# One layer of a hybrid decoder: Winograd block products with both x parts in one 512-column moving operand, and sums moved to GpSimd

## Chip, cores and metric

The kernel runs on one core of one Trainium2 chip. The metric is the device time of the program in microseconds (us); shorter is better. The engines are TensorE (PE, with its weight loads as PEld), VectorE (DVE), ScalarE (ACT), GpSimd (POOL) and SyncE (SP); SP and POOL also issue the DMAs.

## The reference

512 tokens, width 1024, one layer in float32. A mixer (stick-breaking attention and a gated short convolution, merged by two sigmoid gates), a cross-attention into 256 memory tokens, then a SwiGLU feed-forward of hidden size 2816, each with a residual, and a final norm. What the change touches is the projections of the last two sublayers:

```python
q = (h @ w_q).reshape(b, s, MEM_HEADS, MEM_HEAD_DIM)
...
hf = rms_norm(x, norm_ffn[l])
gate, up = jnp.split(hf @ w_ffn_in[l], 2, axis=-1)
x = x + (jax.nn.silu(gate) * up) @ w_ffn_out[l]
```

## The kernel before

**Two parts.** Every float32 operand of a matmul is split in two reduced parts, hi (a cast on ScalarE) and lo (the value less hi, a subtraction on VectorE). A product then takes three matmuls: hi by hi, hi by lo, lo by hi.

**Block products.** Three projections (the last merge gates, the memory queries, the FFN's input weights) use Winograd's scheme for 2x2 blocks: seven products (i = 0 to 6) of block sums instead of eight plain ones. For the FFN, block m of 22 makes 128 gate and 128 up channels for 512 tokens; the four memory-query blocks have numbers QM to QM + 3, the gate blocks start at GM. The x side is split by halves of the tokens (HS = 256 columns) and by pairs of 128-row chunks (four pairs, KP). `odd_forms` and `even_forms` (L605 to L636) make the seven forms of x for a pair, each 256 columns, as hi and lo: three tiles of 512 columns for oh, ch, dh with their lows, and u. The weight side is four raw blocks of 512 columns loaded per m plus sums of them.

**Loads.** `ffn_load(m)` (L712) issues three SP loads (s13, wg, a22) and, on POOL, a DMA that adds two blocks onto s13. `ffn_raw(m, i)` (L729) makes the two remaining sums (i = 3 and 6), each a 128x512 add; its engine is VectorE unless the call says GpSimd, which it does for the few sums ahead of a stage. `ffn_form(m, i)` (L741) casts a raw block on ScalarE and subtracts on VectorE; products 0 and 1 share one of 1024 columns.

**Products and banks.** `product(ps, m, i)` (L768) issues for each of four k three matmuls of 256 columns. The products of one m use three PSUM banks: z for i = 0, 3, 4, 5, v for 1, y for 2 and 6. Products 3 to 6 accumulate onto what is in the bank, so what was there must be read first. `reads(m, i)` (L794) does so: ScalarE copies z after 0, 3 and 4 (and after 5 for memory queries), VectorE adds v or y to a copy. `second(m)` (L807) adds y, as product 2 left it, to the copy of product 4. Half of every bank (256 columns) is used.

**Order.** `order(m0, n)` (L812) interleaves two neighbouring m: (m,3), (m+1,0), (m,4), (m+1,1), (m,5), (m+1,2), (m,6), and so on; the seven products from one such group to the next are called a block here. The FFN loop (L1159 to L1218) is under a manual schedule, in which PE, ACT and DVE run their instructions as written; POOL is not in the list. At step n the loop issues product n, its reads, the form of the product AHEAD = 6 steps on, and the sum of the one SUM_AHEAD = 2 steps further. `evict` (L1107) then multiplies the gate half by the norm's factor (L1111), applies SiLU on ScalarE, and multiplies by the up half, read in two halves from z and from the copy (L1118). Steps with i = 3 and m from 2 to 9 also scale a chunk of x2T for the final residual (L1201). The FFN's output product comes after (L1268), with `turn` products (L1287) over part of it that use `act_forms`.

**Pools.** xpool and upool hold the forms of x; tpool the copies and gate tiles; wpool and fpool the weights. The raw sums and a22 share a ring of four buffers (tag w2).

Of the kernel before, what the change touches and what calls it, by code (L numbers as in the profile page):

```python
# [50 lines left out]
def hybrid_layer(ctx: ExitStack, tc: tile.TileContext, xT_d, memT_d, cols_d, wv_d, win_d,  # L51
# [560 lines left out]
    def odd_forms(u, c, xe, xo, last=None):  # L612
        lo, hi = slice(0, HS), slice(HS, S)
        d = f(unit("c2"))
        oh, ol, ch, cl = (unit(t) for t in ("xoh", "xol", "xch", "xcl"))
        dh, dl = (last or spare)("xdh"), (last or spare)("xdl")
        nc.scalar.copy(oh, xo)
        nc.vector.tensor_tensor(out=c[:, hi], in0=xo[:, hi], in1=xe[:, hi], op=ALU.subtract)
        nc.vector.scalar_tensor_tensor(out=d[:, lo], in0=c[:, lo], scalar=-1.0, in1=xo[:, hi],  # L619
                                       op0=ALU.mult, op1=ALU.subtract)  # L620
# [5 lines left out]
        nc.vector.tensor_tensor(out=cl, in0=c, in1=f(ch), op=ALU.subtract)  # L626
        nc.vector.tensor_tensor(out=dl, in0=d, in1=f(dh), op=ALU.subtract)
        return listed((u[:, lo], u[:, hi]), oh, ol, ch, cl, dh, dl)

# [82 lines left out]
    def ffn_load(m):  # L712

        src = (wfi_d[m] if m < NF else wfp_d[m - NF] if m < QM else wmq_d[m - QM] if m < GM
               else wga_d[m - GM])
        a = src.rearrange("p (i c) -> p i c", i=4)
        s13, wg = ((fpool, "wg") if (m % 3, t) in ((1, "ws"), (2, "wg")) else (wpool, "wr")
                   for t in ("ws", "wg"))
        s13 = s13[0].tile([P, 2, 512], F32, tag=s13[1], name=nm("ws"))
        after(nc.sync.dma_start(s13, a[:, 2:3, :].broadcast_to([P, 2, 512])), x_loads[-1:])  # L720
        wg = wg[0].tile([P, 2, 512], F32, tag=wg[1], name=nm("wg"))
        nc.sync.dma_start(wg, a[:, 0:2, :])
        a22 = fpool.tile([P, 512], F32, tag="w2", name=nm("a22"), bufs=4)
        nc.sync.dma_start(a22, a[:, 3, :])
        nc.gpsimd.dma_start(s13, a[:, 0:4:3, :], accum_op=ALU.add)  # L725
        pairs[m] = wg
        raws[m] = [wg[:, 0, :], wg[:, 1, :], s13[:, 1, :], None, s13[:, 0, :], a22, None]

    def ffn_raw(m, i, eng=nc.vector):  # L729
        if m not in raws:  # L730
            ffn_load(m)
        w = raws[m]
        if w[i] is None:
            w[i] = fpool.tile([P, 512], F32, tag="w2", name=nm("s2"), bufs=4)
            a, b = (w[2], w[0]) if i == 3 else (w[3], w[1])
            eng.tensor_tensor(out=w[i], in0=a, in1=b, op=ALU.add)
        return w[i]
# [30 lines left out]
    def product(ps, m, i, ks=range(KP)):  # L768

        w = wforms[m, i]  # L770
        for k in ks:
            hi, lo = (w[j][:, k * P:(k + 1) * P] for j in range(2))
            xh, xl = (x2f if m < NF else af if m < QM else x1f if m < GM else x0f)[k][i]
            for j, (a, b) in enumerate(((hi, xh), (hi, xl), (lo, xh))):
                nc.tensor.matmul(ps[:, :HS], a, b, start=i < 3 and k == 0 and j == 0,  # L775
                                 stop=k == KP - 1 and j == 2, skip_group_check=True)

    banks, act, silus, stts = {}, {}, [], []

    def bank_of(m, i, new=True):  # L780
        if not new:
            pass
        elif i == 0:
            banks[m] = {"z": ztile("z"), "s": None if m >= GM else tmp("sa"),
                        "t": f(unit("qb")) if QM <= m < GM else tmp("sb")}
        elif i == 1:
            banks[m]["v"] = mmtile("v")
            if m < GM:
                banks[m]["g"] = f(unit("qa")) if m >= QM else tmp("fg")
        elif i == 2:  # L790
            banks[m]["y"] = otile("y")
        return banks[m]["zvyzzzy"[i]]

    def reads(m, i):  # L794

        b = banks[m]
        z, s, t = b["z"][:, :HS], b["s"], b["t"]
        if i in (0, 3, 4) or i == 5 and m >= QM:
            nc.scalar.copy((s[:, :HS], None, None, s[:, HS:], t[:, :HS], t[:, :HS])[i], z)  # L799
        elif i == 1:  # L800
            nc.vector.tensor_tensor(out=b["g"][:, :HS], in0=b["v"][:, :HS], in1=s[:, :HS],
                                    op=ALU.add)
        elif i == 6:
            nc.vector.tensor_tensor(out=b["g"][:, HS:], in0=b["y"][:, :HS], in1=s[:, HS:],
                                    op=ALU.add)

    def second(m):  # L807
        b = banks[m]
        nc.vector.tensor_tensor(out=b["t"][:, HS:], in0=b["y"][:, :HS], in1=b["t"][:, :HS],
                                op=ALU.add)  # L810

# [295 lines left out]
    def evict(m, part):  # L1107
# [6 lines left out]
        else:  # L1114
            a = act[m] = f(unit("act"))
            for half, u in enumerate((b["z"][:, :HS], b["t"][:, HS:])):
                sl = slice(half * HS, (half + 1) * HS)
                stts.append(nc.vector.scalar_tensor_tensor(out=a[:, sl], in0=u, scalar=-1.0,  # L1118
                                                           in1=g[:, sl], op0=ALU.mult,
                                                           op1=ALU.mult))  # L1120

# [37 lines left out]
    with tc.manual_schedule(engines={mybir.EngineType.PE, mybir.EngineType.Activation,  # L1159
                                     mybir.EngineType.DVE}):  # L1160
        ahead = uses[:3] + [(1, 0)]
# [4 lines left out]
        for n, (m, i) in enumerate(uses):  # L1166
            if (m, i) == (1, 0):
                product(banks[m]["z"], m, i, range(KP - 2, KP))
            elif n > 2:
                product(bank_of(m, i), m, i)  # L1170
            if i == 4:
                reads(m, i)
            elif i == 5 and m == NF - 1:
                reads(m, i)
                second(m)
            else:
                if i == 1 and m > 0:
                    second(m - 1)
                reads(m, i)
            if i == 5 and TURN_AT <= m < TURN_AT + KD:  # L1180
# [106 lines left out]
    def turn_product(p, i):  # L1287
# [180 lines left out]
```

## Time and profile before

| | before |
|---|---|
| time of three runs | 2944.97, 846.79, 846.61 us; median 846.79 |
| the profiled execution's own time | 847.03 us |
| its span, first to last instruction | 845.3 us |
| mean granted TensorE clock | 0.997 |
| HBM read, written | 116.42 MB, 2.10 MB |
| FFN products, from the first to the last | about 498 to 724 us |
| memory-query products | about 342 to 383 us |

A profile is one execution. In its rows a tile is named without its buffer number, and a line can be that of a helper that many callers share: the product matmuls of all stages are L775. Durations of neighbouring instructions of one engine overlap a little, so the pitch from start to start says more of the engine's load than the duration. "Idle before" is time that the engine stood still ahead of an instruction, with what ended it.

### The profile page before, as it was taken

The page shows a single profiled execution, that of the slowest core. Times are in us where ns is not written, and L with a number is a line of the kernel's source. Part 1 is how long each engine was busy: PE and PEld are TensorE (multiplying, and loading weights), DVE is VectorE, ACT ScalarE, POOL GpSimd, SP SyncE. Part 2 cuts the span into 40 slices and gives each one's busy share as a digit, 9 for nine tenths or more (in the row PEclk, how much of TensorE's full clock was granted, in tenths as well). Part 3 has the DMA queues.
Part 4 walks back from the last instruction along what each step waited for, and adds up shares of the span by engine and source line. Part 5 has one row for each costly group of instructions (what it writes and reads, how often), then busy time and mean ns, then how long its engine had stood idle before and what let it go on. Part 6 is the DMA issues. An engine that isn't in the chain of part 4 may idle for free.

```text
span 845.3 us, 13478 instructions
## 1 busy us (share of the span) xinstructions
PE 835.7 (99%) x5095; PEld 748.2 (89%) x5095; DVE 669.3 (79%) x1152; ACT 482.9 (57%) x873; POOL 88.5 (10%) x113
## 2 busy tenths in 40 slices
PE   9999999999999999999999999999999999999996
PEld 7888787888899988999988899999999999888885
DVE  8769889987856867978775889888877778895764
ACT  7556767566534555766554766555455556554434
POOL 1011112210100011000000111211111110110013
PEclk9999999999999999999999999999999999999998
DMA  8332332314745484555331437777777763870112
GB/s 299 128 122 64 108 104 66 111 51 167 206 104 146 148 251 128 162 178 194 129 115 56 112 86 202 189 185 177 179 182 178 180 156 125 269 216 26 51 50 100
DMA packets 50257, 120.47 MB, mean 143 GB/s; under 512 B 5136, under 2 KB 8208, under 8 KB 50192
## 3 DMA queue, kind: packets, MB, share of 16 engines
q1 hardware_dynamic: 40656, 101.49, 36.2%
q0 software_dynamic: 9248, 17.83, 13.0%
q8 instruction: 40, 0.66, 0.3%
q10 hardware_dynamic: 288, 0.29, 0.1%
q14 instruction: 25, 0.20, 0.1%
HBM read 116.42 MB, written 2.10 MB: 140 GB/s over the span
## 4 chain that ended last, share of the span: by engine, by line
PE 99%; DVE 0%; ACT 0%; issue 0%; DVEq 0%; ACTq 0%
PE z L775 20%; PE y L775 10%; PE pr L176 6%; PE pr L177 6%; PE pr L178 6%; PE v L775 5%; PE r L176 3%; PE r L178 3%; PE r L177 3%; PE f L177 3%; PE f L176 3%; PE f L178 3%; PE v L282 3%; PE br L177 2%; PE br L176 2%; PE br L178 2%
## 5 line engine op out<-in xcount | busy, mean ns | idle before, releaser
L167 ACT CAST wh<-wr 128x1024 fp32r<-128x1024 f32 x82 | 85.6, 1048 | 51.8 <-PE pr L177 11.3
L170 DVE TENSOR_TENSOR wl<-wr,wh 128x1024 fp32r<-128x1024 f32 x82 | 99.9, 1222 | 18.7 <-ACT wh L167 17.9
L775 PE MATMUL z<-xdh,wf 128*128 128x256 f32 x480 | 94.6, 282 | 0.0
L176 PE MATMUL pr<-xgh,wh 128*128 128x512 f32 x224 | 87.8, 392 | 0.0
L178 PE MATMUL pr<-xgh,wl 128*128 128x512 f32 x224 | 87.3, 390 | 0.0
L177 PE MATMUL pr<-xgl,wh 128*128 128x512 f32 x224 | 87.3, 390 | 0.0
L775 PEld LDWEIGHTS z<-xdh,wf 128*128 128x128 f32 x480 | 77.5, 189 | 0.3 <-issue 0.2
L775 PE MATMUL z<-xdl,wf 128*128 128x256 f32 x240 | 67.0, 279 | 0.0
L799 ACT COPY sa<-z 128x256 f32<-128x256 f32 x52 | 19.4, 373 | 74.1 <-PE z L775 74.0
L766 DVE TENSOR_TENSOR wf<-s,wf 128x512 fp32r<-128x512 f32 x60 | 41.4, 691 | 22.8 <-ACT wf L765 21.6
L725 POOL DMA_DIRECT2D ws<-in_w_ffn_in_dram x22 | 26.5, 1203 | 299.0 <-DVE c L619 109.5
L752 DVE TENSOR_TENSOR wf<-wg,wf 128x1024 fp32r<-128x1024 f32 x30 | 36.8, 1226 | 18.1 <-ACT wf L749 18.1
L178 PEld LDWEIGHTS pr<-xgh,wl 128*128 128x128 f32 x224 | 42.0, 188 | 8.9
L176 PEld LDWEIGHTS pr<-xgh,wh 128*128 128x128 f32 x224 | 42.1, 188 | 8.6 <-DVE rv L135 0.3
L177 PEld LDWEIGHTS pr<-xgl,wh 128*128 128x128 f32 x224 | 42.1, 188 | 8.3
L775 PE MATMUL y<-xch,wf 128*128 128x256 f32 x240 | 49.0, 286 | 0.0
L775 PE MATMUL z<-xch,wf 128*128 128x256 f32 x240 | 48.1, 283 | 0.0
L775 PEld LDWEIGHTS z<-xdl,wf 128*128 128x128 f32 x240 | 45.4, 189 | 0.2
L177 PE MATMUL f<-wl,acth 128*128 128x512 f32 (+1 forms) x116 | 44.3, 382 | 0.0
L176 PE MATMUL f<-wh,acth 128*128 128x512 f32 (+1 forms) x116 | 44.3, 382 | 0.0
L178 PE MATMUL f<-wh,actl 128*128 128x512 f32 (+1 forms) x116 | 44.1, 382 | 0.0
L766 DVE TENSOR_TENSOR wf<-ws,wf 128x512 fp32r<-128x512 f32 x60 | 40.9, 682 | 1.4 <-ACT wf L765 1.3
(357 smaller groups left out, 2466.3 us busy)
## 6 DMA issues: line engine op xcount, KB each, us to landing
wr<-in_w_in_dram SPq DMA_DIRECT2D x28, 512.0 KB, 3.5
ws<-in_w_ffn_in_dram SPq DMA_DIRECT2D x22, 512.0 KB, 3.8
ws<-in_w_ffn_in_dram POOLq DMA_DIRECT2D x22, 512.0 KB, 5.8
wg<-in_w_ffn_in_dram SPq DMA_DIRECT2D x22, 512.0 KB, 4.2
wr<-in_w_ffn_out_dram SPq DMA_DIRECT2D x14, 512.0 KB, 4.4
a<-in_w_ffn_in_dram SPq DMA_DIRECT2D x22, 256.0 KB, 4.4
wr<-in_w_branch_dram SPq DMA_DIRECT2D x8, 512.0 KB, 3.5
wr<-in_w_mix_out_dram SPq DMA_DIRECT2D x8, 512.0 KB, 3.7
```

What stands on the lines that cost most here:

```text
L167: after(nc.scalar.copy(h2, raw), lead[-1:] + waiting[:1])
L170: lows.append(nc.vector.tensor_tensor(out=l2, in0=raw, in1=f(h2), op=ALU.subtract))
L176: nc.tensor.matmul(ps, a[0], b[0], start=start, stop=False, **kw)
L177: nc.tensor.matmul(ps, a[0], b[1], start=False, stop=False, **kw)
L178: nc.tensor.matmul(ps, a[1], b[0], start=False, stop=stop, **kw)
L282: nc.tensor.matmul(vps[t], xg[k][a][:, sl], wv[k][b], start=k == 0 and (a, b) == (0, 0), stop=k == KD - 1 and a == 1)
L725: nc.gpsimd.dma_start(s13, a[:, 0:4:3, :], accum_op=ALU.add)
L752: nc.vector.tensor_tensor(out=lo, in0=pair, in1=f(hi), op=ALU.subtract)
L766: nc.vector.tensor_tensor(out=lo, in0=raw, in1=f(hi), op=ALU.subtract)
L775: nc.tensor.matmul(ps[:, :HS], a, b, start=i < 3 and k == 0 and j == 0, stop=k == KP - 1 and j == 2, skip_group_check=True)
L799: nc.scalar.copy((s[:, :HS], None, None, s[:, HS:], t[:, :HS], t[:, :HS])[i], z)
```

## The change

`odd_forms` lays every form of x out as one 512-column tile: hi in the left half, lo in the right; it casts and subtracts in six pieces of 256 columns. `product` then issues, for FFN and memory queries, one matmul of hi with the whole 512 columns and one of lo with the 256 of xh. So the bank's left half holds hi xh + lo xh and its right half hi xl, and the two halves must be added. `reads` copies or adds banks at their full width into two-part tiles (g2 for the gate half, t2 for the up half, of the new pool twopool; z is now copied after product 5 too), and `fold` adds left and right halves on GpSimd. `evict` takes the folded up half in one instruction. The FFN's weight sums move from VectorE to GpSimd. POOL enters the FFN's manual schedule: the load of m + 2 stands at (m,1), sum 3 of m + 1 at (m,2), sum 6 of m + 2 at (m,6). The a22 load is issued apart, when its form comes near. The last two lines make the buffer that POOL's DMAs use smaller. The gate blocks keep three matmuls; the turn products use the first two entries of a form.

```diff
+    twopool = ctx.enter_context(tc.tile_pool(name="twopool", bufs=1))
...
     def odd_forms(u, c, xe, xo, last=None):
         lo, hi = slice(0, HS), slice(HS, S)
         d = f(unit("c2"))
-        oh, ol, ch, cl = (unit(t) for t in ("xoh", "xol", "xch", "xcl"))
-        dh, dl = (last or spare)("xdh"), (last or spare)("xdl")
-        nc.scalar.copy(oh, xo)
+        forms = [u] + [(unit if i in (1, 2, 4, 6) else last or spare)("xf") for i in range(1, 7)]
+        src = [None, xo[:, lo], c[:, lo], d[:, lo], c[:, hi], d[:, hi], xo[:, hi]]
+
+        def his(*some):
+            for i in some:
+                nc.scalar.copy(forms[i][:, lo], src[i])
+
+        def los(*some):
+            for i in some:
+                nc.vector.tensor_tensor(out=forms[i][:, hi], in0=src[i], in1=f(forms[i][:, lo]),
+                                        op=ALU.subtract)
+
+        his(1, 6)
...
-        nc.scalar.copy(ch, c)
-        nc.vector.tensor_tensor(out=ol, in0=xo, in1=f(oh), op=ALU.subtract)
+        his(2, 4)
+        los(1, 6)
...
-        nc.scalar.copy(dh, d)
-        nc.vector.tensor_tensor(out=cl, in0=c, in1=f(ch), op=ALU.subtract)
-        nc.vector.tensor_tensor(out=dl, in0=d, in1=f(dh), op=ALU.subtract)
-        return listed((u[:, lo], u[:, hi]), oh, ol, ch, cl, dh, dl)
+        his(3, 5)
+        los(2, 4, 3, 5)
+        return [(u[:, lo], u[:, hi], u) for u in forms]
...
     def ffn_load(m):
...
-        a22 = fpool.tile([P, 512], F32, tag="w2", name=nm("a22"), bufs=4)
-        nc.sync.dma_start(a22, a[:, 3, :])
...
+        corners[m] = a[:, 3, :]
+        if m >= NF:
+            corner(m)
+
+    def corner(m):
+        a22 = raws[m][5] = fpool.tile([P, 512], F32, tag="w2", name=nm("a22"), bufs=4)
+        nc.sync.dma_start(a22, corners[m])
...
     def product(ps, m, i, ks=range(KP)):
...
-            xh, xl = (x2f if m < NF else af if m < QM else x1f if m < GM else x0f)[k][i]
+            start, stop = i < 3 and k == 0, k == KP - 1
+            if m < GM:
+                xh, _, x = (x2f if m < NF else x1f)[k][i]
+                nc.tensor.matmul(ps, hi, x, start=start, stop=False, skip_group_check=True)
+                nc.tensor.matmul(ps[:, :HS], lo, xh, start=False, stop=stop,
+                                 skip_group_check=True)
+                continue
+            xh, xl = x0f[k][i]
...
+    def add_bank(part, ps):
+        nc.vector.tensor_tensor(out=part, in0=ps, in1=part, op=ALU.add)
+
+    def fold(m, s, s2):
+
+        ps = s2.rearrange("p h (j t) -> p h j t", j=2)
+        u = banks[m][s] = tmp("fg") if m < NF else f(unit("q" + s))
+        nc.gpsimd.tensor_tensor(out=u.rearrange("p (h t) -> p h t", h=2), in0=ps[:, :, 0, :],
+                                in1=ps[:, :, 1, :], op=ALU.add)
+
     def reads(m, i):
...
-        z, s, t = b["z"][:, :HS], b["s"], b["t"]
-        if i in (0, 3, 4) or i == 5 and m >= QM:
-            nc.scalar.copy((s[:, :HS], None, None, s[:, HS:], t[:, :HS], t[:, :HS])[i], z)
+        if i in (0, 4):
+            s = "g2" if i == 0 else "t2"
+            b[s] = twopool.tile([P, 2, 512], F32, tag=s, name=nm(s), bufs=2 if i == 0 else 1)
+        if i in (0, 3, 4, 5):
+            s, h = (("g2", 0), None, None, ("g2", 1), ("t2", 1), ("t2", 0))[i]
+            nc.scalar.copy(b[s][:, h, :], b["z"])
         elif i == 1:
-            nc.vector.tensor_tensor(out=b["g"][:, :HS], in0=b["v"][:, :HS], in1=s[:, :HS],
-                                    op=ALU.add)
+            add_bank(b["g2"][:, 0, :], b["v"])
         elif i == 6:
-            nc.vector.tensor_tensor(out=b["g"][:, HS:], in0=b["y"][:, :HS], in1=s[:, HS:],
-                                    op=ALU.add)
+            add_bank(b["g2"][:, 1, :], b["y"])
+            fold(m, "g", b["g2"])
+        if i == 5:
+            b["read"] = True
+            if "second" in b:
+                fold(m, "t", b["t2"])
 
     def second(m):
         b = banks[m]
-        nc.vector.tensor_tensor(out=b["t"][:, HS:], in0=b["y"][:, :HS], in1=b["t"][:, :HS],
-                                op=ALU.add)
+        add_bank(b["t2"][:, 1, :], b["y"])
+        if "read" in b:
+            fold(m, "t", b["t2"])
+        b["second"] = True
...
-            for half, u in enumerate((b["z"][:, :HS], b["t"][:, HS:])):
-                sl = slice(half * HS, (half + 1) * HS)
-                stts.append(nc.vector.scalar_tensor_tensor(out=a[:, sl], in0=u, scalar=-1.0,
-                                                           in1=g[:, sl], op0=ALU.mult,
-                                                           op1=ALU.mult))
+            stts.append(nc.vector.scalar_tensor_tensor(out=a, in0=b["t"], scalar=-1.0, in1=g,
+                                                       op0=ALU.mult, op1=ALU.mult))
...
     with tc.manual_schedule(engines={mybir.EngineType.PE, mybir.EngineType.Activation,
-                                     mybir.EngineType.DVE}):
+                                     mybir.EngineType.DVE, mybir.EngineType.Pool}):
...
+            if i == 1 and m > 0:
+                second(m - 1)
             elif i == 5 and m == NF - 1:
...
+            if i == 1 and 1 < m + 2 < NF:
+                ffn_load(m + 2)
+            reads(m, i)
+            if i == 2 and m + 1 < NF:
+                ffn_raw(m + 1, 3, nc.gpsimd)
+            elif i == 6 and m + 2 < NF:
+                ffn_raw(m + 2, 6, nc.gpsimd)
...
-                ffn_raw(*uses[n + AHEAD + SUM_AHEAD])
+                ffn_raw(*uses[n + AHEAD + SUM_AHEAD], nc.gpsimd)
...
-            x = [u[:, t * P:(t + 1) * P] for u in af[p][i]]
+            x = [u[:, t * P:(t + 1) * P] for u in af[p][i][:2]]
...
-    nc = bacc.Bacc("TRN2", target_bir_lowering=False, num_devices=1)
+    nc = bacc.Bacc("TRN2", target_bir_lowering=False, num_devices=1,
+                   dynamic_dma_scratch_size=4096)
```

More of the change, by code (lines that the diff above doesn't have):

```diff
@@ L732, in ffn_raw @@
         w = raws[m]
+        if w[i] is None and i == 5:
+            corner(m)
         if w[i] is None:
@@ L772, in product @@
             hi, lo = (w[j][:, k * P:(k + 1) * P] for j in range(2))
[L773 removed]
+            start, stop = i < 3 and k == 0, k == KP - 1
[6 more added lines that the diff above has]
+            xh, xl = x0f[k][i]
             for j, (a, b) in enumerate(((hi, xh), (hi, xl), (lo, xh))):
[L775 to L776 removed]
+                nc.tensor.matmul(ps[:, :HS], a, b, start=start and j == 0, stop=stop and j == 2,
+                                 skip_group_check=True)
     banks, act, silus, stts = {}, {}, [], []
```

17 lines of the change are left out of this document (5 added, 12 removed).

## The prediction

> **What bounds the kernel now.** I read the page first, then the chain as pieces in time, then the engines' rows in one block of the FFN stage.
>
> ```profile
> span 845.3 us, 13478 instructions
> PE 835.7 (99%) x5095; PEld 748.2 (89%) x5095; DVE 669.3 (79%) x1152; ACT 482.9 (57%) x873; POOL 88.5 (10%) x113
> PE z L775 20%; PE y L775 10%; PE pr L176 6%; PE pr L177 6%; PE pr L178 6%; PE v L775 5%; PE r L176 3%; PE r L178 3%; PE r L177 3%; PE f L177 3%; PE f L176 3%; PE f L178 3%; PE v L282 3%; PE br L177 2%; PE br L176 2%; PE br L178 2%
> ```
>
> TensorE is busy for 835.7 of 845.3 us, and the block products (z, y and v of L775) carry 35% of the chain. So now the time is TensorE's, and a shorter product shortens it, provided that no other engine becomes the limit. The products of one FFN block, in the chain:
>
> ```profile
> 563.08 4.29 PE z L775 x36
> 567.37 1.44 PE v L775 x12
> 568.81 1.42 PE z L775 x12
> 570.23 2.87 PE y L775 x24
> 573.10 4.29 PE z L775 x36
> ```
>
> From z to z are 84 matmuls in 573.10 - 563.08 = 10.02 us: 28 triples of 0.358 us, 0.119 us for each 256-column matmul. The granted clock is full, and VectorE is the next busiest:
>
> ```profile
> core 0: us, PE busy (x) PEld busy (x) DVE busy (x) ACT busy (x) POOL busy (x), PEclk, DMA share, GB/s
> 518.10:548.20 30.10, 30.10 (x254) 30.10 (x254) 27.37 (x49) 17.14 (x32) 6.43 (x7) 1.00 0.74 183
> 598.50:648.50 50.00, 50.00 (x423) 50.00 (x422) 38.57 (x69) 26.88 (x52) 6.01 (x5) 1.00 0.73 183
> 342.40:388.00 45.60, 45.60 (x381) 45.37 (x380) 39.63 (x69) 31.65 (x60) 2.41 (x2) 1.00 0.58 174
> ```
>
> VectorE fills 91% of an early FFN stretch, 77% of a late one and 87% of the memory-query stage. Its room decides what the change is worth.
>
> **TensorE's part of the change.** A triple (hi with xh, hi with xl, lo with xh) becomes one matmul of 512 columns and one of 256. The columns stay at 768; one matmul goes. The price of 512 columns stands in the output stage:
>
> ```profile
> 739.73 0.39 PE L176 MATMUL f<-wh,acth 128*128 128x512 f32 x1
> ...
> 741.77 0.39 PE L176 MATMUL f<-wh,acth 128*128 128x512 f32 x1
> ```
>
> Nine steps lie between these rows: 2.04 / 9 = 0.227 us. A triple becomes 0.2267 + 0.1193 = 0.346 instead of 0.358, 0.0119 less. A block becomes 28 x 0.346 = 9.69 us. The 22 FFN blocks have 616 triples, the four memory-query blocks 112: 728 x 0.0119 = 8.7 us, of which 7.3 in the FFN. This is all that the change can bring. By the Trainium skill (TensorE: Matmul & The Clock Gate, section "Wait — 56ns, not 53.3ns?") a warm matmul costs its columns at 2.4 GHz and about 2.5 ns. By that rule, 728 matmuls fewer would be worth only 1.8 us. The two steps of the trace give 2 x 0.1193 - 0.2267 = 0.0119 us of fixed cost per matmul, and the trace decides.
>
> **What the other engines get.** One FFN block on VectorE:
>
> ```profile
> 629.41 1.23 DVE L752 TENSOR_TENSOR wf<-wg,wf 128x1024 fp32r<-128x1024 f32 x1 [0.63 <-ACT wf L749]
> 630.55 0.42 DVE L809 TENSOR_TENSOR sb<-y,sb 128x256 f32<-128x256 f32 x1
> 630.89 0.41 DVE L801 TENSOR_TENSOR fg<-v,sa 128x256 f32<-128x256 f32 x1
> 631.22 0.68 DVE L766 TENSOR_TENSOR wf<-ws,wf 128x512 fp32r<-128x512 f32 x1
> 631.82 0.42 DVE L1118 SCALAR_TENSOR_TENSOR act<-z,fg 128x256 f32<-128x256 f32 x1
> ...
> 632.49 0.68 DVE L766 TENSOR_TENSOR wf<-a,wf 128x512 fp32r<-128x512 f32 x1
> 633.09 0.68 DVE L736 TENSOR_TENSOR s<-s,wg 128x512 f32<-128x512 f32 x1
> 634.17 0.42 DVE L804 TENSOR_TENSOR fg<-y,sa 128x256 f32<-128x256 f32 x1 [0.40 <-PE y L775]
> ```
>
> Back to back, starts lie 0.60 us apart after 512 columns (631.22 to 631.82), 1.14 after 1024 and 0.34 after 256. With these pitches VectorE's own block is before: weight forms 1.14 + 5 x 0.60, two weight sums 1.20, the product with r0b (L1111, 512 columns) 0.60, three PSUM adds 1.02, two act halves 0.68, together 7.64. After: forms 4.14, r0b 0.60, one act product 0.60, three PSUM adds of 512 columns 1.83 (0.61, from the last fence of this part), together 7.17. The two sums (L736) leave it. Of the 7.17, 5.34 are instructions with both inputs in SBUF.
>
> GpSimd gets four adds of 128x512 a block: two sums, two folds. Their price, and what they do to VectorE:
>
> ```profile
> L725 POOL DMA_DIRECT2D ws<-in_w_ffn_in_dram x22 | 26.5, 1203 | 299.0 <-DVE c L619 109.5 <-DMA ws<-in_w_ffn_in_dram 104.7 <-DVE s L736 36.5
> L1378 POOL TENSOR_TENSOR yt<-yt,gain 128x512 f32<-128x512 f32 x7 | 9.0, 1289 | 77.5 <-ACT sq L1376 77.5
> ```
>
> ```profile
> 220.49 1.29 POOL L736 TENSOR_TENSOR s<-ws,wg 128x512 f32<-128x512 f32 x1 [9.05 <-PE br L178]
> ...
> 316.71 2.18 POOL L736 TENSOR_TENSOR s<-ws,wg 128x512 f32<-128x512 f32 x1 [8.06 <-DMA ws<-in_w_mem_q_dram]
> ...
> 481.19 2.59 POOL L736 TENSOR_TENSOR s<-ws,wg 128x512 f32<-128x512 f32 x1 [5.36 <-DMA ws<-in_w_ffn_in_dram]
> ```
>
> ```profile
> 220.51 1.82 DVE L191 TENSOR_TENSOR xdl<-c,xdh 128x512 fp32r<-128x512 f32 x1
> ...
> 317.65 1.52 DVE L608 TENSOR_TENSOR c<-xr 128x256 f32<-128x256 f32 x1
> ...
> 481.94 0.68 DVE L626 TENSOR_TENSOR xcl<-c,xch 128x512 fp32r<-128x512 f32 x1
> 482.54 0.68 DVE L672 TENSOR_TENSOR x<-r,x 128x512 f32<-128x512 f32 x1
> 483.23 1.10 DVE L627 TENSOR_TENSOR xdl<-c,xdh 128x512 fp32r<-128x512 f32 x1
> ...
> 826.31 0.69 DVE L1374 TENSOR_TENSOR yt<-f,yt 128x512 f32<-128x512 f32 x1 [1.62 <-PE f L178]
> 826.92 0.61 DVE L1334 SCALAR_TENSOR_TENSOR fv<-ss,epst 128x1 f32<-128x1 f32 x1
> ```
>
> This is what speaks against the change. While GpSimd adds, a VectorE instruction with two SBUF inputs stands still: xdl took 1.82 instead of 0.69, c took 1.52 instead of 0.41. One add blocks for 1.13 or 1.11, say 1.12 us. In the third case GpSimd waited through xcl, got in beside x<-r, whose first input is in PSUM and which kept its 0.68, and cost the next xdl only 1.10 - 0.69 = 0.41. So an add beside PSUM reads is cheap. By the Trainium skill (SBUF — State Buffer, section "Who interferes with whom") a VectorE instruction with two SBUF inputs contends with a GpSimd instruction that reads SBUF, whichever comes first blocks the other for its whole length, and one with a single SBUF input doesn't contend. The trace agrees; whole lengths would be 4 x 1.29 instead of 4 x 1.12 a block.
>
> Four adds hold the port for 4.48 us. If none is covered, VectorE needs 7.17 + 4.48 = 11.65 us a block; if every PSUM add covers (1.83), 9.82. Walking the written order, the fold of t comes ready after the (m,5) copy, while VectorE, when late, is at its two neighbouring PSUM adds (second and v): covered. Sum 3, fold g (ready only when the y add is done) and sum 6 then fall among form subtractions: 7.17 + 3.36 = 10.53. If GpSimd gets in only beside PSUM reads, as at 482.54, it is nearer 9.82. I take the middle, 10.2. Either way that is over TensorE's 9.69: **VectorE with its blocked time becomes the bound.** Blocks 2 to 9 also scale x2T on VectorE, another 512 columns at a pitch of 0.60, so 10.8:
>
> ```profile
> L1201 DVE TENSOR_TENSOR x<-x,rms 128x512 f32<-128x512 f32 x5 | 3.4, 685 | 0.0
> ```
>
> FFN: before 22 x 10.02 = 220.4; after 14 x 10.2 + 8 x 10.8 = 229.2, so +8.8. Once, VectorE may fall behind without harm: the add of second(m-1) comes two products ahead of product (m-1,6), which accumulates onto the same bank: -2 x 1.38 = -2.8. FFN: +6.0.
>
> Memory query: TensorE -1.3. Eight folds could block 9.0 there, and the twelve PSUM adds grow by 12 x 0.27 = 3.2, against 45.60 - 39.63 = 6.0 us idle: between -1.3 and +6.2. With half the folds beside PSUM reads it fits nearly; I take 0.
>
> Costed at nothing: ScalarE's bank copies (four of 512 columns instead of three of 256).
>
> ```profile
> 631.30 0.59 ACT L1141 COPY yt<-xt 128x512 f32<-128x512 f32 x1 [0.88 <-PE xt L1138]
> ...
> 635.59 0.37 ACT L799 COPY sa<-z 128x256 f32<-128x256 f32 x1 [2.66 <-PE z L775]
> ```
>
> They add 4 x 0.59 - 3 x 0.37 = 1.25 us to a ScalarE busy for 26.88 of 50. A copy must end within the one product (1.38) before the bank is accumulated again; behind it wait the weight casts, then the form subtractions, and TensorE six products later. The odd forms as six pieces of 256 instead of three of 512 cost VectorE 6 x 0.34 - 3 x 0.60 = 0.24 for each of 12 pairs, 2.9 us if the residual stages' matmuls didn't hide it.
>
> ```profile
> ws<-in_w_ffn_in_dram SPq DMA_DIRECT2D x22, 512.0 KB, 3.8
> ws<-in_w_ffn_in_dram POOLq DMA_DIRECT2D x22, 512.0 KB, 5.8
> ...
> a<-in_w_ffn_in_dram SPq DMA_DIRECT2D x22, 256.0 KB, 4.4
> ```
>
> The accumulating DMA (1.20 on POOL) now stands in POOL's order ahead of the fold of t and behind sum 6 of the block before, some four products later (5.5 us); its input takes 3.8 us to land and its buffers have been free since the block before, so POOL shouldn't wait. Its 5.8 us end well ahead of sum 3, nine products on. The a22 load, moved behind the next block's two loads on SP, waits for a sum's buffer, which its form leaves five products before the a22 cast: 6.9 us for 4.4. If VectorE is late by over 2.5 us, that cover is gone too, and ScalarE waits for the rest.
>
> Sum: 847.03 of the profiled run (845.3 and 1.7 around it) + 6.0 + 0 = 853.0; the median is 846.79, so **853**.
>
> **Rivals.** *Everything hides* (0.23): the adds fall into VectorE's idle time (11.4 of 50 us late in the FFN) and beside PSUM reads, TensorE stays the bound: 846.8 - 8.7 = 838. For it: 9.82 is only just over 9.69. Against it: blocks 2 to 9, and that the idle pieces of the block above are 0.63 and 0.40 us, shorter than an add. *Blocked throughout* (0.27): adds alternate with form subtractions, as at 317.65, and late folds and casts leave gaps between; the block is midway between 10.53 and 11.65, 11.1: 14 x 11.1 + 8 x 11.7 - 220.4 - 2.8 = +25.8, so 873. It decides once fewer than two of the four adds lie beside PSUM reads. Its end, nothing covered and 6.2 in the memory query, is 14 x 11.65 + 8 x 12.25 - 220.4 - 2.8 + 6.2 = +44, 891. *GpSimd's queue as the bound* (0.05): 4 x 1.29 + 1.20 = 6.36 us a block, and it needs over 3.3 us of waiting for the port to exceed 9.69; then sums come late to the casts. At a 1024-column form's 1.14 for each add it is 10.92: 22 x 10.92 - 220.4 - 2.8 = +17, 864.
>
> **How the numbers follow.** My forecast (0.45) reaches from 843 (9.82 a block and -1.3) to 860 (10.53). With the hidden case below and most of the blocked one above, 838 to 875 leaves out about 2 in 10. A measurement of this kernel tells 2% from no change, 830 to 864 here: faster 0.02 (the only gain is 8.7 us), same 0.68 (the forecast and the hidden case), slower 0.30 (the blocked case and about half of GpSimd's queue).
>
> **What would show it.** Right: product steps near 0.346 a triple where TensorE doesn't wait; TensorE idle in the FFN, waiting for VectorE's y add or forms; VectorE's L766 and L752 means above 0.69 and 1.23; GpSimd adds over 1.29. Wrong: L766 near 0.69 and blocks of 9.7 us (hidden), blocks of 11 us (blocked), or TensorE waiting for bank copies instead.

## The result, and the profile after

The changed kernel takes 887.83 us (median of four runs, 886.24 to 888.95) against 847.1 of the kernel before beside it: a ratio of 1.0481, 95% interval 1.0456 to 1.0507. The forecast was 853, the range 838 to 875. The profiled execution took 888.77 us; its span is 41.5 us longer than before's. From the page of the kernel after: the span, the engines' busy time, the chain's shares, and four groups (busy us, mean ns of one, idle time before them).

```profile
span 886.8 us, 12263 instructions
PE 845.6 (95%) x4367; PEld 714.4 (81%) x4367; DVE 741.3 (84%) x1123; ACT 512.2 (58%) x931; POOL 242.0 (27%) x208
PE 69%; DVE 20%; issue 6%; POOL 2%; ACT 2%; DMA 1%; DVEq 0%; SPq 0%; ACTq 0%
L785 DVE TENSOR_TENSOR wf<-s,wf 128x512 fp32r<-128x512 f32 x60 | 62.9, 1050 | 9.1 <-issue 6.8
L785 DVE TENSOR_TENSOR wf<-ws,wf 128x512 fp32r<-128x512 f32 x60 | 57.9, 964 | 1.6 <-ACT wf L784 1.5
L755 POOL TENSOR_TENSOR s<-ws,wg 128x512 f32<-128x512 f32 x24 | 43.0, 1794 | 21.3 <-DMA ws<-in_w_gates_dram 8.2
L826 POOL TENSOR_TENSOR fg<-g 128x512 f32<-128x512 f32 x22 | 37.8, 1716 | 38.9 <-DVE g L820 38.9
```

VectorE has 29 instructions fewer than before and is busy 72 us longer. Its form subtractions (L785) take 1.05 and 0.96 us on average where one took 0.68 before, and GpSimd's sums and folds of g 1.79 and 1.72 us, where an undisturbed add took 1.29: each side holds the other up. The chain now lies on VectorE for a fifth of the span.

Where the 41.5 us arise is read from the chain. First the kernel before, then the kernel after: the end of the memory-query stage (`var`), the first and the last product of the FFN, and between them a piece near the FFN's end. Columns: start, us, what.

```profile
388.66 0.79 PE var L209 x8
...
498.13 1.07 PE z L775 x9
...
722.97 1.47 PE y L775 x12
```

```profile
396.55 0.79 PE var L210 x8
...
505.99 0.23 PE z L795
...
746.89 1.67 POOL fg L826
748.56 1.72 POOL s L755
...
750.29 3.12 DMA a<-in_w_ffn_in_dram
...
768.56 0.12 PE y L796
```

The memory query ends 7.9 us later. The FFN starts 7.9 us later, so nothing is added between. FFN products last from 505.99 to 768.68, 262.7 us, against 498.13 to 724.44, 226.3: +36.4. The tail is 118.1 us against 120.9, -2.7: some of the output stage's products now run among the late FFN products. 7.9 + 36.4 - 2.7 = 41.6, the 41.5 of the spans but for rounding.

Inside the FFN, the form that opens each block shows the pace. Two of them 17 blocks apart, before and after, from VectorE's timeline:

```profile
528.84 1.31 DVE L752 TENSOR_TENSOR wf<-wg,wf 128x1024 fp32r<-128x1024 f32 x1
...
702.65 1.23 DVE L752 TENSOR_TENSOR wf<-wg,wf 128x1024 fp32r<-128x1024 f32 x1 [0.63 <-ACT wf L749]
```

```profile
545.08 1.21 DVE L771 TENSOR_TENSOR wf<-wg,wf 128x1024 fp32r<-128x1024 f32 x1
...
740.10 1.21 DVE L771 TENSOR_TENSOR wf<-wg,wf 128x1024 fp32r<-128x1024 f32 x1
```

195.02 us against 173.81: 21.2 of the 36.4 us come from these 17 blocks at their steady pace, the other 15.2 from the stage's beginning and end: from the first product to the first of these forms are 39.1 us against 30.7, from the second form to the last product 28.6 against 21.8.

The blocks before are not all alike. From form to form they take 10.02 us up to 618.95 and 10.46 from there on, because TensorE also makes four transposes of 128 columns (of x2T, for the final residual) in each of the later ones. In the chain of the kernel before:

```profile
620.36 0.44 PE xt L1138 x4
```

The kernel after has blocks of 11.82 us up to 627.83 and 11.22 behind, so the change costs 1.80 us in an early block and about 0.76 in a late one. One steady block on VectorE, whole (columns: start, us, engine, line, operation):

```profile
640.18 0.68 DVE L820 TENSOR_TENSOR t<-y,t 128x512 f32<-128x512 f32 x1
640.78 0.67 DVE L820 TENSOR_TENSOR g<-v,g 128x512 f32<-128x512 f32 x1
641.38 1.47 DVE L785 TENSOR_TENSOR wf<-ws,wf 128x512 fp32r<-128x512 f32 x1
642.77 1.78 DVE L1159 SCALAR_TENSOR_TENSOR act<-fg,fg 128x512 f32<-128x512 f32 x1
644.48 0.68 DVE L785 TENSOR_TENSOR wf<-a,wf 128x512 fp32r<-128x512 f32 x1
645.08 0.68 DVE L820 TENSOR_TENSOR g<-y,g 128x512 f32<-128x512 f32 x1
645.68 0.68 DVE L785 TENSOR_TENSOR wf<-ws,wf 128x512 fp32r<-128x512 f32 x1
646.28 1.78 DVE L785 TENSOR_TENSOR wf<-s,wf 128x512 fp32r<-128x512 f32 x1
648.73 1.00 DVE L785 TENSOR_TENSOR wf<-s,wf 128x512 fp32r<-128x512 f32 x1 [0.67 <-issue]
649.65 0.68 DVE L1154 TENSOR_TENSOR fg<-fg,r0b 128x512 f32<-128x512 f32 x1
650.26 1.21 DVE L771 TENSOR_TENSOR wf<-wg,wf 128x1024 fp32r<-128x1024 f32 x1
651.39 0.68 DVE L820 TENSOR_TENSOR t<-y,t 128x512 f32<-128x512 f32 x1
```

GpSimd in the same block:

```profile
641.01 1.29 POOL L826 TENSOR_TENSOR fg<-t 128x512 f32<-128x512 f32 x1 [1.90 <-DVE t L820]
642.27 1.73 POOL L755 TENSOR_TENSOR s<-ws,wg 128x512 f32<-128x512 f32 x1
...
645.83 1.67 POOL L826 TENSOR_TENSOR fg<-g 128x512 f32<-128x512 f32 x1 [1.83 <-DVE g L820]
647.47 1.71 POOL L755 TENSOR_TENSOR s<-s,wg 128x512 f32<-128x512 f32 x1
```

A block takes 651.39 - 640.18 = 11.21 us. VectorE's own work in it is 7.17, as predicted. Four instructions are longer than their 0.68: 0.79, 1.10, 1.10 and 0.32, together 3.31, one beside each GpSimd add. Of the 0.73 that remain, 0.67 is idle time. In it VectorE stands behind ScalarE:

```profile
647.54 0.59 ACT L837 COPY g<-z 128x512 f32<-128x512 f32 x1 [2.43 <-POOL fg L826]
648.02 0.62 ACT L784 CAST wf<-s 128x512 fp32r<-128x512 f32 x1
648.54 0.59 ACT L837 COPY t<-z 128x512 f32<-128x512 f32 x1
```

The copy of z waits until GpSimd has read one of the two g2 buffers (fold of g, 645.83 + 1.67 = 647.50). Behind it, in ScalarE's written order, stand the cast that the subtraction at 648.73 needs and the other bank copy, after which TensorE may accumulate. So TensorE's longest sum of waits names ScalarE although VectorE and GpSimd set the pace (us in total, times, longest):

```profile
PE z L795 <- ACT t L837: 16.7, 19, 1.1
```

### The profile page after: what moved, and what is told of

It is laid out like the page before. It is cut to its first block, busy times and chain, and to the rows that moved or that the text cites. A ratio compares the mean times of both kernels' runs of the same rounds, so it can differ in the third digit from the quotient of the medians.

```text
span 886.8 us, 12263 instructions
## 1 busy us (share of the span) xinstructions
PE 845.6 (95%) x4367; PEld 714.4 (81%) x4367; DVE 741.3 (84%) x1123; ACT 512.2 (58%) x931; POOL 242.0 (27%) x208
## 4 chain that ended last, share of the span: by engine, by line
PE 69%; DVE 20%; issue 6%; POOL 2%; ACT 2%; DMA 1%; DVEq 0%; SPq 0%; ACTq 0%
DVE wf L785 8%; PE pr L177 6%; PE pr L179 6%; PE pr L178 6%; PE r L179 3%; PE r L178 3%; PE r L177 3%; PE f L178 3%; PE f L179 3%; PE f L177 3%; DVE g L820 3%; DVE wf L771 3%; PE z L801 3%; PE z L795 3%; PE v L283 2%
## 5 line engine op out<-in xcount | busy, mean ns | idle before, releaser
L795 PE MATMUL z<-xf,wf 128*128 128x512 f32 x416 | 153.5, 406 | 17.0 <-ACT t L837 16.7
L796 PE MATMUL z<-xf,wf 128*128 128x256 f32 x416 | 118.2, 284 | 0.0
L795 PEld LDWEIGHTS z<-xf,wf 128*128 128x128 f32 x416 | 79.8, 192 | 41.9 <-ACT t L837 22.7
L795 PE MATMUL y<-xf,wf 128*128 128x512 f32 x208 | 76.7, 405 | 6.7 <-DVE t L820 6.6
L837 ACT COPY g<-z 128x512 f32<-128x512 f32 x52 | 30.4, 585 | 87.5 <-PE z L796 42.7
L796 PEld LDWEIGHTS z<-xf,wf 128*128 128x128 f32 x416 | 80.3, 193 | 0.2
L785 DVE TENSOR_TENSOR wf<-s,wf 128x512 fp32r<-128x512 f32 x60 | 62.9, 1050 | 9.1 <-issue 6.8
L785 DVE TENSOR_TENSOR wf<-ws,wf 128x512 fp32r<-128x512 f32 x60 | 57.9, 964 | 1.6 <-ACT wf L784 1.5
L796 PE MATMUL y<-xf,wf 128*128 128x256 f32 x208 | 58.2, 280 | 0.0
L795 PEld LDWEIGHTS y<-xf,wf 128*128 128x128 f32 x208 | 39.0, 188 | 18.8 <-DVE t L820 10.4
L755 POOL TENSOR_TENSOR s<-ws,wg 128x512 f32<-128x512 f32 x24 | 43.0, 1794 | 21.3 <-DMA ws<-in_w_gates_dram 8.2
L826 POOL TENSOR_TENSOR fg<-g 128x512 f32<-128x512 f32 x22 | 37.8, 1716 | 38.9 <-DVE g L820 38.9
L826 POOL TENSOR_TENSOR fg<-t 128x512 f32<-128x512 f32 x22 | 29.1, 1324 | 64.4 <-DVE t L820 49.0
```

The lines of the kernel that those rows point to most:

```text
L785: nc.vector.tensor_tensor(out=lo, in0=raw, in1=f(hi), op=ALU.subtract)
L795: nc.tensor.matmul(ps, hi, x, start=start, stop=False, skip_group_check=True)
L796: nc.tensor.matmul(ps[:, :HS], lo, xh, start=False, stop=stop, skip_group_check=True)
L826: nc.gpsimd.tensor_tensor(out=u.rearrange("p (h t) -> p h t", h=2), in0=ps[:, :, 0, :], in1=ps[:, :, 1, :], op=ALU.add)
L837: nc.scalar.copy(b[s][:, h, :], b["z"])
```

## The experiments

Three theories stood against each other. **P**: GpSimd's adds and VectorE's instructions with two SBUF inputs hold each other up. **R**: the adds end late, and the bank copies wait for one of two g2 buffers. **W**: the doubled width is too much work for ScalarE and VectorE, whoever does the adds. Each time is compared with the kernel before on the same chip: 846.46 us beside the first four, 846.96 beside the next four, 846.54 beside the last two.

**1. The FFN's sums on VectorE, the folds left on GpSimd.**

```diff
-                ffn_raw(m + 1, 3, nc.gpsimd)
+                ffn_raw(m + 1, 3)
...
-                ffn_raw(m + 2, 6, nc.gpsimd)
+                ffn_raw(m + 2, 6)
...
-                ffn_raw(*uses[n + AHEAD + SUM_AHEAD], nc.gpsimd)
+                ffn_raw(*uses[n + AHEAD + SUM_AHEAD])
```

> The changed kernel with the FFN's weight sums on VectorE again; only the two folds of a block stay on GpSimd. Theory P (the shared port: an add on GpSimd holds up VectorE's instructions with two SBUF inputs): VectorE's own block is 7.17 + 1.20 = 8.37 us, the fold of t lies largely beside PSUM adds, the fold of g blocks about 1.1, so 9.5 to 10.4 a block instead of 11.2, and the time is 840 to 858 us. Theory R (the ring of two g2 buffers: the fold of g comes late, ScalarE waits with its bank copy for the buffer, TensorE waits for ScalarE): the fold of g stands at the same place, so about 880 to 888. Theory W (the wider copies and adds themselves cost it, GpSimd has no part in it): 888 or a little more.

Measured: 871.72 us (871.11 to 871.98), ratio 1.0297 (1.028 to 1.0314). Giving VectorE two more instructions a block makes the kernel 16.1 us faster, which is P's direction and not R's; the size is outside both ranges. The two folds that stay show why, in VectorE's timeline of this kernel:

```profile
642.89 1.49 DVE L785 TENSOR_TENSOR wf<-ws,wf 128x512 fp32r<-128x512 f32 x1
...
647.31 1.78 DVE L785 TENSOR_TENSOR wf<-ws,wf 128x512 fp32r<-128x512 f32 x1
```

They still cost 0.81 and 1.10 us, since I had counted the fold of t as covered. 7.17 + 1.20 + 1.91 = 10.28; the block takes 10.60.

**2. All four adds on VectorE.** The three lines above, and the fold:

```diff
-        nc.gpsimd.tensor_tensor(out=u.rearrange("p (h t) -> p h t", h=2), in0=ps[:, :, 0, :],
+        nc.vector.tensor_tensor(out=u.rearrange("p (h t) -> p h t", h=2), in0=ps[:, :, 0, :],
```

> The changed kernel with sums and folds all on VectorE; GpSimd has no add in the FFN and the memory queries. P: nothing is blocked; VectorE's block is 7.17 + 1.20 + 1.20 = 9.57 us, just under TensorE's 9.69, and with waits 9.7 to 10.2: 838 to 852 us. R: the fold follows the y add at once, so the ring is free early: also 838 to 852. W: 888 or more, since VectorE has 2.4 us more a block.

Measured: 858.70 us (858.64 to 859.2), ratio 1.0145 (1.013 to 1.0161). W falls as the main cause: the same widths without GpSimd's adds are 29.1 us faster, and 12.2 us over the kernel before are left to the widths and VectorE's added work. The late blocks take 10.18 us. VectorE's own work in them is 9.57, and TensorE is busy for all of the 40 us from 640 on: with its 28 triples and the four transposes, TensorE is the bound here again. The early blocks take 10.28, where VectorE has 9.57 + 0.60. The result is 6.7 us over P's range, and that much is lost before the FFN, in this kernel's chain:

```profile
396.03 0.79 PE var L210 x8
```

The memory query ends 7.4 us later than before's 388.66 with no add on GpSimd. Run 10 takes this up.

**3. A third g2 buffer.** Room comes from one buffer of upool and a smaller DMA scratch.

```diff
-            b[s] = twopool.tile([P, 2, 512], F32, tag=s, name=nm(s), bufs=2 if i == 0 else 1)
+            b[s] = twopool.tile([P, 2, 512], F32, tag=s, name=nm(s), bufs=3 if i == 0 else 1)
```

> The changed kernel with three g2 buffers instead of two (to find room, one unit buffer less and a smaller buffer for POOL's DMAs). P: only the 0.67 us for which VectorE stood idle behind ScalarE in each block goes; VectorE stays the bound at about 10.5 (11.1 in blocks 2 to 9): 868 to 878 us. R: ScalarE no longer waits for the fold, blocks fall to about 9.7 to 9.9: 840 to 850. W: unchanged, 888.

Measured: 886.69 us (one run). R falls, and P's number too. VectorE, at the place where the kernel after had its idle 0.67:

```profile
645.55 3.49 DVE L785 TENSOR_TENSOR wf<-s,wf 128x512 fp32r<-128x512 f32 x2
```

The wait is gone, and the second of the pair, which it had kept partly clear of GpSimd's sum, is now held up in full: two instructions with a pitch of 0.60 take 3.49, 1.10 more each. The block is 11.25 us, against 11.21. TensorE's longest sum of waits, 16.7 us behind ScalarE's copies in the kernel after, is now 21.1 us behind VectorE's `t L820`. In the steady block the ring of two was a symptom.

**4. GpSimd only writes.** Folds and FFN sums become memsets of the same tiles, so the kernel leaves these sums out.

```diff
+            if m < NF and eng is nc.gpsimd:
+                eng.memset(w[i], 0.125)
...
-        nc.gpsimd.tensor_tensor(out=u.rearrange("p (h t) -> p h t", h=2), in0=ps[:, :, 0, :],
-                                in1=ps[:, :, 1, :], op=ALU.add)
+        nc.gpsimd.memset(u, 0.125)
```

> The changed kernel with the FFN's weight sums and all folds replaced by GpSimd memsets of the same tiles (so these sums are left out of the computation). GpSimd has as many instructions but reads nothing. P, with the port shared for reads: VectorE 7.17 a block, TensorE the bound at 9.69, and the time is 836 to 842 us; this also tells what the wider matmul is worth alone. If writes hold the port as well, VectorE is blocked for the memsets' time, 4 x 0.5 a block, which still fits: 838 to 845. R: 836 to 842 too, since nothing waits for a fold. W: 880 to 888.

Measured: 840.23 us (one run), 6.2 below before. Copies, VectorE's wide adds, the pool of two buffers and the order of the loads all stay, and TensorE bounds the kernel again; the memory query ends 1.0 us earlier than before. So the wide product by itself is worth some 6 us, and the adds, four a block and the memory query's eight folds, cost 887.83 - 840.23 = 47.6 where the change puts them.

**5 and 6. The kernel before, with four idle GpSimd instructions a block** from m = 2 on, working on a tile that nothing else uses: adds in the fifth run, memsets in the sixth. No wide product, no fold, no wide copy; in both, POOL is in the manual schedule and its DMAs' buffer is the smaller one.

```diff
+    dum = cpool.tile([P, 2, 512], F32, tag="dum", name="dum")
+    nc.gpsimd.memset(dum, 0.5)
...
+        if 1 < m < NF:
+            for _ in range(4):
+                nc.gpsimd.tensor_tensor(out=dum[:, 1, :], in0=dum[:, 0, :], in1=dum[:, 0, :], op=ALU.add)
```

> The kernel before, unchanged in its products, with four more GpSimd adds (128x512, both inputs and the output in a tile that nothing else uses) behind the accumulating DMA of each FFN block from 2 on, and POOL in the manual schedule. Nobody waits for these adds. P: they come in a burst, 4 x 1.1 us of blocked time against the 2.4 us that VectorE has left in a 10.0 us block (7.64 of its own); with what falls beside its PSUM adds a block becomes 10.8 to 12, and 20 such blocks make 862 to 887 us. R and any theory in which the wait for GpSimd's results costs the time: 847. W (the wide tiles): 847.

Measured: 884.00 us (one run). GpSimd's group, then VectorE beside it:

```profile
623.62 5.85 POOL L732 TENSOR_TENSOR dum<-dum 128x512 f32<-128x512 f32 x4
```

```profile
623.78 1.90 DVE L1206 TENSOR_TENSOR x<-x,rms 128x512 f32<-128x512 f32 x1
625.61 1.52 DVE L771 TENSOR_TENSOR wf<-s,wf 128x512 fp32r<-128x512 f32 x1
627.06 1.52 DVE L1116 TENSOR_TENSOR fg<-fg,r0b 128x512 f32<-128x512 f32 x1
628.50 2.06 DVE L757 TENSOR_TENSOR wf<-wg,wf 128x1024 fp32r<-128x1024 f32 x1
```

Each add lengthens one VectorE instruction by 0.8 to 1.2 us, whatever its line. No instruction reads what they write, and still they cost 37.0 us. Not all of it is blocked time. The four blocks from 534.42 to 594.01 take 13.8 to 16.9 us, over P's 12, and hold 19.6 of the 37.0; POOL's DMAs ran late at their beginning too (ScalarE waits 3.50 us for one at 539.69). How these blocks' excess divides is open. The 13 behind them take 11.2 on average, as P has it.

> The same as the run before it in the list, but the four added GpSimd instructions are memsets of 128x512, which read nothing. P, with the port shared for reads alone: 847, VectorE's subtractions keep 0.68. If GpSimd's writes or its mere activity held VectorE up: 850 to 865.

Measured: 847.48 us (one run), no change. VectorE, while GpSimd is busy with its four memsets:

```profile
628.20 0.69 DVE L771 TENSOR_TENSOR wf<-s,wf 128x512 fp32r<-128x512 f32 x1 [0.74 <-ACT wf L770]
```

So P is shown on the kernel before alone, and it is GpSimd's reading that counts. The rule of the Trainium skill that the prediction weighed (SBUF — State Buffer, section "Who interferes with whom") says this as well: a VectorE instruction with two SBUF inputs contends with a GpSimd instruction that reads SBUF, not with one that only writes. The trace agrees, 0.69 beside memsets against 1.52 beside adds.

Two inputs are not needed in every case. In the kernel after, a cast with one SBUF input runs beside GpSimd's sums:

```profile
520.45 1.48 DVE L202 CAST acch<-acc 128x512 fp32r<-128x512 f32 x1
```

It took 0.42 in the kernel before, as did the scaling `eps_sq<-rms`, which takes 1.51 here. So the prediction's words that an instruction with a single SBUF input doesn't contend go too far. The sentence of the Trainium skill (SBUF — State Buffer, section "Who interferes with whom") that they shorten excepts VectorE's 2-port modes; whether these two ran in one, no row says. The PSUM adds, for which the prediction needed it, do keep their pace: 0.67 at 640.78, beside the fold.

**7 and 8. Part of the gain without GpSimd.** On the kernel before: in run 7 the wide product only for i = 1, 2 and 6, whose banks VectorE reads anyway; the right half is added by a second instruction from PSUM. In run 8 only for i = 0, 3, 4 and 5, whose banks ScalarE copies; folds and sums on VectorE. The memory query is left as it was.

```diff
+            if m < NF and i in (1, 2, 6):
+                nc.tensor.matmul(ps, hi, x[0], start=i < 3 and k == 0, stop=False,
+                                 skip_group_check=True)
+                nc.tensor.matmul(ps[:, :HS], lo, xh, start=False, stop=k == KP - 1,
+                                 skip_group_check=True)
+                continue
...
+        if m < NF:
+            nc.vector.tensor_tensor(out=out, in0=ps[:, HS:], in1=out, op=ALU.add)
```

> The kernel before with the 512-column product only for the FFN's products 1, 2 and 6 (banks v and y), and the right bank half added on VectorE straight from PSUM, 256 columns, three instructions more a block; no GpSimd add, sums on VectorE, memory queries as before. P: VectorE's block is 7.64 + 3 x 0.34 = 8.66, under TensorE's 9.9, so TensorE stays the bound and gives 12 x 22 triples x 0.010 = 2.6 us: 843 to 845. W: three wide products in seven cost up to half of the change's loss: 860.

Measured: 847.00 us (11 runs, 846.37 to 847.71), ratio 1.0001 (0.9992 to 1.001): nothing gained. Two of the chain's v products in this kernel:

```profile
629.29 0.23 PE v L784
...
630.35 0.23 PE v L784
```

Three triples lie between them, 0.353 each, which would make 264 x 0.0045 = 1.2 us; why it is 0.348 in the next run stays open. The blocks show more: 9.91 us early and about 10.34 late, 2.2 us less than before over the 17 blocks. The FFN's beginning takes it back: from the first product to the form that opens m = 4 are 33.5 us against 30.7. VectorE, already busy for 9.90 of the 10 us from 510 on in the kernel before, has three more adds a block there, and TensorE is busy for 28.6 of the 30 us from 510 on, against all 30 before.

```diff
+            if m < NF and i in (0, 3, 4, 5):
...
+        nc.vector.tensor_tensor(out=u.rearrange("p (h t) -> p h t", h=2), in0=ps[:, :, 0, :],
+                                in1=ps[:, :, 1, :], op=ALU.add)
```

> The kernel before with the 512-column product only for the FFN's products 0, 3, 4 and 5 (bank z), copied at full width by ScalarE, v and y added at 256 columns, two folds of 512 columns a block on VectorE, sums on VectorE, memory queries as before. P: VectorE's block is 8.76 (9.36 in blocks 2 to 9) against TensorE's 9.85; TensorE gives 16 x 22 x 0.010 = 3.5 us: 843 to 846, less if VectorE's waits of 0.6 us a block, as in the run with everything on VectorE, push it over in blocks 2 to 9. W: wide copies cost: 860 or more.

Measured: 845.27 us (11 runs, 844.82 to 846.66), ratio 0.9984 (0.9975 to 0.9993). This version beats both kernels, by 1.7 and by 42.6 us. Its z products in the chain:

```profile
623.27 0.23 PE z L785
...
624.66 0.23 PE z L785
```

Four triples in 1.39 us, 0.348 each. The blocks take 9.85 us early and 10.30 late, and VectorE, with 44.77 us busy in the 50 from 598.5 on, has a little room left. The 17 blocks gain 3.5 us; the FFN's beginning, 33.6 us against 30.7, takes most of that back.

**9. The folds on VectorE, the sums left on GpSimd,** the other half of run 2 (its second diff alone).

> The changed kernel with the folds on VectorE and the weight sums left on GpSimd, the opposite split to the run with sums on VectorE. The runs so far make theory P additive: VectorE's own pitches plus about 1.1 us for each GpSimd add that doesn't begin beside a PSUM read. Both sums follow no PSUM read in the written order, so 7.17 + 1.20 + 2.2 = 10.6 us a block (11.2 in blocks 2 to 9), and with the 2 to 3 us that the changed kernel lost beyond its 22 blocks and 7 us of the memory queries, 870 to 878 us. If instead only the folds, on which other instructions wait, did the harm, the sums would hide: 855 to 860.

Measured: 873.12 us (one run). Against the kernel after, run 1 gains 16.1, this one 14.7, both together (run 2) 29.1: the parts nearly add up, and neither fold nor sum is the culprit alone. The sum that meets the 1024-column form, in this kernel's VectorE timeline:

```profile
642.50 2.31 DVE L771 TENSOR_TENSOR wf<-wg,wf 128x1024 fp32r<-128x1024 f32 x1
```

2.31 - 1.23 = 1.08 us: the hold-up is the add's, and doesn't grow with the instruction that it meets.

**10. Run 2 with the memory query narrow again,** as the kernel before has it, and the a22 load and the order of POOL's instructions as before too.

```diff
+            if m < NF and i < 7:
+                nc.tensor.matmul(ps, hi, x[0], start=i < 3 and k == 0, stop=False,
+                                 skip_group_check=True)
...
+        if m < NF:
+            return wide_reads(m, i)
```

> Sums and folds all on VectorE, as in the run that did so, but the memory queries keep three matmuls, 256-column copies and adds and no folds. If that stage's loss of 7 us is VectorE's own added work there (eight folds of 0.60 and twelve PSUM adds wider by 0.27, 8.0 us against 6.0 us idle), it goes: 850 to 853 us. If it comes from elsewhere (the forms in six pieces, the smaller buffer for POOL's DMAs), it stays: 858 to 860.

Measured: 850.13 us (850.06 to 851.74), ratio 1.0047 (1.0031 to 1.0064), 8.6 less than run 2. The end of the memory query in its chain:

```profile
387.77 0.79 PE var L210 x8
```

That is 8.3 us before run 2's 396.03, so nearly the whole gain is in that stage: there the wide product costs more than it brings, wherever its folds run. The 3.6 us over the kernel before that remain come mainly from the FFN's beginning, 35.3 us against 30.7; the 17 blocks behind it are 0.4 us shorter than before's.

## Why the prediction was wrong, point by point

**Right: the bound.** VectorE with its blocked time sets the pace, and the steady block is between the prediction's ends, 9.82 and 11.65. Right too are VectorE's own 7.17 us, the price of one add (1.10 in the block above, 1.12 predicted), the 0.60 more for blocks 2 to 9 (11.82 against 11.21), and GpSimd's queue: 6.40 of adds and 1.20 of DMA issue a block, well under the block's length.

**Failed: "the fold of t comes ready after the (m,5) copy, while VectorE, when late, is at its two neighbouring PSUM adds (second and v): covered."** The fold reads what `second` writes. In the block above it waits for `DVE t L820` and starts at 641.01, when the first of the two adds has ended and only some 0.4 us of the second is left. It then holds up the next subtraction by 0.79. The other three adds fall among two-SBUF-input instructions, as in the walk, if not all beside the form subtractions (the act product is one of those held up; the 1024-column form, which I expected to lengthen, is so only once among the FFN's 22, 1.72 at 502.09, and takes 1.21 or 1.22 otherwise); the last one is paid for as 0.67 of waiting and 0.32 of blocking. So the walk should have given 7.17 + 4 x 1.1, less some 0.4 of cover: 11.2.

**Failed: "I take the middle, 10.2."** There was no reason in the traces for going below the walk towards 9.82: one of three earlier adds had got in beside a PSUM read, and that was taken for a habit. In the steady block every add met a two-SBUF-input instruction. By the prediction's own test, "once fewer than two of the four adds lie beside PSUM reads", the blocked rival was the likely case; it was given 0.27, and its end, 891, is close to what came.

**Failed: memory query at 0.** It came to +7.9, above its upper bound of 6.2. Run 2 has +7.4 there without any add on GpSimd, run 10 has none. The stage's 6.0 us of idle VectorE time isn't slack that can be filled: in run 2, 3.2 for wider adds and 8 x 0.60 for folds are 8.0 us of plain work, and about as much comes out. That the two match is in part chance: the chain of run 2 there also passes a DMA (`wr<-in_w_mem_k_dram`, 6.49 us at 373.39) that follows VectorE's last sum. In the kernel after, blocked time stands in the folds' place, 1.48 and 1.78 us at 355.05 and 359.46 for instructions of 0.68.

**Failed: the one-time slack of -2.8, and a22 at nothing.** The stage's beginning and end cost 15.2 us instead of winning some, 8.4 and 6.8. At the end, the chain above goes from a fold over a sum to the a22 load, 3.12 us of a DMA that waited for the sum's buffer: the cover of 2.5 us that the prediction named was gone. At the beginning stand the norm's instructions, held up too (L202 and L203 in the chain, 1.42 and 1.65). There was no slack there to fall behind in: VectorE was full before the change, and the beginning is long in every kernel that gives it more, 35.8 us in run 2, while in run 4, without the adds, it is 30.9. How the 15.2 us divide among these causes was not measured apart.

**Smaller than predicted: TensorE's gain.** A triple takes 0.348 instead of 0.346, so 728 x 0.010 = 7.3 in place of 8.7, and run 4 shows 6.2. The rule of the Trainium skill set beside it (TensorE: Matmul & The Clock Gate, section "Wait — 56ns, not 53.3ns?") would have made it 1.8, by estimate; the trace stays with 0.010 a matmul. **Held: the odd forms** in six pieces stand in run 4 as well, where the memory query ends 1.0 us earlier than before and the FFN's beginning is 0.2 longer; that leaves little room for 2.9 us.

**Left out: the late blocks' transposes.** The prediction took the block before as 10.02 us throughout, and TensorE's block after as 9.69. In the late blocks the transposes make that 10.46 and 10.13, or 10.18 as run 4 measured, so TensorE alone needs there what was forecast for VectorE. Since VectorE came to 11.2, this did not decide the time.

The ledger, measured less predicted: 17 steady blocks 21.2 - (10 x 10.2 + 7 x 10.8 - 17 x 10.02) = +13.9 (the blocks after 17.4 longer than forecast, those before 3.5 longer than 10.02 each); the FFN's beginning and end 15.2 - (4 x 10.2 + 10.8 - 5 x 10.02 - 2.8) = +16.5; the memory query +7.9; the tail -2.7. Together 35.6 of the 888.77 - 853.0 = 35.8 us.

## What to carry to other kernels

An add moved from a loaded VectorE to GpSimd is not off VectorE: here it cost 0.60 us a piece where it was, and about 1.1 as blocked time where it went, so before moving it, count VectorE's instructions with two SBUF inputs (and see whether its casts are held up too), and take an add as covered only if what it waits for lets it start before the cover does. When a walk through the written order gives a number, forecast by the walk and not by a mean with the hopeful end. A wait that a trace puts first (here a ring of two buffers) may be only where the lateness comes to rest; giving it a buffer moved the stall and left the time.

## What the runs showed of the hardware

TensorE runs some stretches after stalls at half its rate. In the kernel after, from the view of stretches (us, busy time of PE, PEld, DVE, ACT and POOL, granted clock, DMA share, GB/s):

```profile
515.00:524.00 9.00, 6.47 (x36) 5.18 (x35) 7.90 (x8) 3.69 (x6) 4.37 (x3) 1.00 0.18 60
524.00:529.00 5.00, 5.00 (x21) 4.30 (x20) 4.93 (x7) 2.82 (x5) 4.12 (x3) 0.66 0.47 157
```

In the second stretch TensorE doesn't wait at all, and yet the clock is 0.66: the chain's 512-column steps there take 0.43 us instead of 0.23 for some 3.4 us. That is about 0.34 x 5 = 1.7 us of TensorE's time. The clock is 0.57 over the 4 us from 756.5 and from 548.5 too. The stretches from 524 and 756.5 take at most some 3.4 of the 15.2 us at the stage's beginning and end, by estimate; the one from 548.5 falls in a block of 11.85 us, no longer than those behind it, since VectorE sets the pace there. In a table of the Trainium skill (TensorE: Matmul & The Clock Gate, Part 1) TensorE has a full and a half rate, and falls to half after at least one idle window of about 3.4 us. The two step lengths agree with the rates. Ahead of the stretch from 524 TensorE waited 1.42 and 1.11 us with one matmul between; whether that made up such a window, this trace doesn't show.
